# A hybrid attention layer on one core: the order of queries' and shares' parts, silu by tanh, and two products on GpSimd

## The chip, the core and the metric

The kernel runs on one NeuronCore of one Trainium2 chip. TensorE (PE) multiplies matrices into PSUM; VectorE (DVE), ScalarE (ACT) and GpSimd (POOL) work on tiles; SyncE (SP) issues most DMAs. Every engine has its own in-order queue of instructions; engines wait for one another on semaphores. The metric is the device time of one execution, in microseconds (us). Lower is better.

## The reference: what is computed

One encoder layer over 512 tokens and 16 learned "meta" tokens (528 rows), model width 2048, all in fp32:

```
hn   = RMSNorm(h); proj = hn @ w_in
qa, ka, va, ga, qb, kb, vb, gb = split(proj)
# mixer A: 8 query heads of 128 on 2 key/value heads
q, k = rope(rmsnorm(qa)), rope(rmsnorm(ka))
oA   = softmax(q k' / sqrt(128)) va
# mixer B: 8 heads, differential attention, two streams of 64
a    = softmax(s1 - slope*dist) - lambda * softmax(s2 - slope*dist)
oB   = rmsnorm(a vb) * (1 - lambda_init)
y    = concat(oA * silu(ga), oB * silu(gb)) @ w_out
out  = h + rmsnorm(y)             # real tokens only
```

silu(x) is x / (1 + exp(-x)), which equals (tanh z + 1) z with z = x / 2.

## The kernel before

**Precision by parts.** Every fp32 operand of a large product is split in two fp32r parts: a high part, which ACT writes as a copy (`hi`, L348), and a low part, which DVE writes as the difference (`lo`, L351). A product is then three matmuls: high by high, low by high, high by low (`three`, L198). The weights go through the same split in blocks of 128x1024 (`wsplit`, L153: tiles `st` to `wh`, `wl`).

**Stages.** (1) The first columns, with x arriving. (2) Mixer B: for each head h the columns of its gate, and the values, keys and queries of head h + 1 (`dense_T`, L224; tiles `pd` in four rotating PSUM banks), with the attention of head h woven in between. (3) Mixer A: its keys, values and two groups of queries. (4) The eight gates of mixer A, with the attention of mixer A woven in. (5) The output product (tiles `po`), with fewer products by sums and differences of blocks, the norm and the residual.

**What sets the order.** On PE the order is the program's. Class `Lanes` (L42) keeps a planned clock, to which every matmul adds its estimate. Work that waits for other engines is written as generators that yield a lag, such as `LAG["scB"]` = 3.0 us between two score products, and `poll` resumes one when the planned clock has passed its time; `finish` forces a task to its end. So the lags decide after which dense products an attention product stands. On ACT, DVE, POOL and SP the compiler's scheduler chooses the order by its own plan, by program order as priority. Splits of weights have a higher priority. Two things bind it: data dependences, and holds: `with tc.issue_after(i):` puts every instruction of the block that is on the engine of `i` behind `i` in that engine's queue. A hold adds no wait of its own; the instruction just cannot be placed earlier in its queue.

**Attention of mixer B** (`attention_B`, L516). For each block of 128 queries and each of two streams PE computes scores into the one PSUM tile `sc` from the queries' high part q and low part l and the keys' tile s, which holds the keys' high part in one half and the low part in the other. DVE adds the distance term, takes the extremum and empties `sc` (L533, tile mx). ACT takes Exp and the sum (L541), POOL scales the first stream (L546), DVE adds the second (L548) and turns blocks of 32x32 (L460). Two blocks of queries make a tile `pt`, which goes through DRAM and comes back regrouped (`regroup`, L464) as `pl`: the shares of attention, "p". `p_times_v` (L477) splits p into `ph` (ACT; one buffer) and `pl` (DVE) and the meta tokens' small `pm`, yields a lag (6.0 us in mixer B, 5.0 in A), and multiplies by the values into `pv`. ACT copies the result out (L554, L647). `finish_B` (L560) squares it, sums by PE, takes a square root on ACT (L573) and four reciprocals on DVE (L578), each 128x128 and held behind the newest maximum; then DVE multiplies the output by the roots (L581) and by the gate (L582), and SP stores it to the scratch `oscr` (L584). `queries_B` (L387) writes the queries' tiles: four high parts on ACT, four low parts on DVE, each of 64 partitions.

**Attention of mixer A** (`attention_A`, L609) is alike with one stream (scores L632 to L634, mxA L636, Exp L639, POOL L641); its queries' parts qh and qlA are written from a PSUM tile of transposes (L617, L618). The gate of head h - 1 is multiplied and stored while the gates' columns of later heads run (`silu_A`, L595; `gate_A`, L601); L602 is the product with the gate, L603 the store.

**Gates.** DVE multiplies the columns by the rows' norms (L437, L597), ACT applies Silu (L438, L598). Where ACT changes between functions of different tables, the compiler puts an ACT_TABLE_LOAD ahead.

Of the kernel before, what the change touches and what calls it, by code (L numbers as in the profile page):

```python
# [10 lines left out]
F32 = mybir.dt.float32  # L11
# [95 lines left out]
def kernel(ctx: ExitStack, tc: tile.TileContext, xT, xn, xm, w_s, w_t, w_q, w_o,  # L107
# [240 lines left out]
    def hi(dst, src):  # L348
        nc.scalar.activation(dst, src, AF.Copy)  # L349

    def lo(dst, src, h):  # L351
        nc.vector.tensor_tensor(out=dst, in0=src, in1=h.bitcast(F32), op=ALU.subtract)  # L352

    def keys_B(pss, after=nullcontext):
# [4 lines left out]
        with after():  # L359
            hi(s1[L], kf[L])  # L360
            hi(s2[U], kf[U])
            lo(s1[U], kf[L], s1[L])
            lo(s2[L], kf[U], s2[U])
# [22 lines left out]

    def queries_B(h, pss, after=nullcontext):  # L387
# [9 lines left out]
        with after():  # L397
            hi(to[0][L], qf[L])
            hi(to[2][U], qf[U])
            hi(to[0][U], qf[L])  # L400
            hi(to[2][L], qf[U])
            lo(to[1][L], qf[L], to[0][L])
            lo(to[3][U], qf[U], to[2][U])
            lo(to[1][U], qf[L], to[0][L])
            lo(to[3][L], qf[U], to[2][U])
# [28 lines left out]

    def gate(pss, name):
        g = gp.tile([P, SEQ], F32, name=name, tag="g", bufs=4)
        nc.vector.tensor_tensor(out=g, in0=pss[0], in1=rB[:, NM:], op=ALU.mult)  # L437
        nc.scalar.activation(g, g, AF.Silu)  # L438
        return g
# [37 lines left out]
    def p_times_v(regrouped, v, done, gate_of):  # L477
# [8 lines left out]
        with tc.issue_after(splits[-1][0].ins):  # L486
            hi(ph, pt)
            hi(pm[0:32], pf)
        lo(pl, pt, ph)
# [26 lines left out]
    def attention_B(h, qs, ks, v, v_task):  # L516
        o = ap.tile([P, SEQ], F32, name="oB", tag="f", bufs=4)
        last = None
        for half in range(2):
# [36 lines left out]
            if half == 0:  # L556
                yield LAG["scB"]
        over[h] = lanes.spawn(finish_B(h, o), LAG["fin"], last)

    def finish_B(h, o):  # L560
# [13 lines left out]
        for t in range(TT):  # L574
# [4 lines left out]
            if t == 1:  # L579
                yield LAG["scB"]  # L580
        nc.vector.tensor_tensor(out=o, in0=o, in1=sq, op=ALU.mult)  # L581
# [13 lines left out]
    def silu_A(pss):  # L595
        g = gp.tile([P, SEQ], F32, name="gt", tag="gt")
        nc.vector.tensor_tensor(out=g, in0=pss[0], in1=rB[:, NM:], op=ALU.mult)  # L597
        nc.scalar.activation(g, g, AF.Silu)  # L598
        return g

    def gate_A(h, g):  # L601
        nc.vector.tensor_tensor(out=oA[h], in0=oA[h], in1=g, op=ALU.mult)  # L602
# [6 lines left out]
    def attention_A(h, qn, q_task, k, k_task, v, v_task):  # L609
# [7 lines left out]
        hi(dealt(qh), by_token(tr))  # L617
        lo(dealt(ql), by_token(tr), dealt(qh))  # L618
# [5 lines left out]
        for half in range(2):  # L624
            pt = ap.tile([P, 1088], F32, name="pt", tag="pt")
            for t in (2 * half, 2 * half + 1):
# [12 lines left out]
                nc.scalar.activation(p, p, AF.Exp, scale=-1.0, bias=mx, accum_out=sm)  # L639
# [235 lines left out]
    heads, over = [None] * (2 * NH), [None] * (2 * NH)  # L875
# [5 lines left out]
    for h in range(NH):  # L881
# [7 lines left out]
        if h + 1 < NH:  # L889
            pss = dense_T(KEYS)  # L890
            if h:
                weigh()
                finish_head(h - 1)
# [369 lines left out]
```

## Time and profile before

| | us |
|---|---|
| runs shown: median (lowest to highest) | 899.06 (898.26 to 902.3) |
| the profiled execution, its own time | 901.28 |
| its span, first to last instruction | 899.5 |
| PE busy | 870.3 |
| DVE busy | 631.4 |
| ACT busy | 497.9 |
| POOL busy | 124.9 |

The granted clock of PE was 0.997 of full speed over the span. A row of a timeline reads: start, duration, engine, source line, operation, output<-inputs, shapes, count; in brackets the idle time of the engine before it and what ended it. A "q" behind an engine (SPq) is its sequencer. Names of tiles leave out the buffer's number, and a helper's line (L61, L349, L352) stands for all that call it, so the tile says which work it is. A matmul's end is modelled and overlaps the next one's start.

### The profile page before, as it was taken

Reading aid. Unit: us, or ns where it says so; the run is one execution under the profiler, and the core shown is the slowest. Engines: PE = TensorE matmul, PEld = TensorE weight load, DVE = VectorE, ACT = ScalarE, POOL = GpSimd, SP = SyncE. Lnnn points to the kernel's source line nnn. Section 1 sums busy time; section 2 is a strip of 40 time slices with the busy share of each in tenths; the row PEclk is TensorE's granted clock in tenths of the full one; section 3 lists DMA queues with packets and bytes.
Section 4 is the critical chain, followed back from the end, with each engine's and each line's share of the span. In section 5 each row is a group of like instructions: output and inputs, shape, how many; then the busy total and the mean of one; then the engine's idle time right before and its main releaser. Section 6 shows DMA issues by size and latency. Waiting matters only on the chain. (4 is left out here: it accounts for less than half of the span.)

```text
span 899.5 us, 14066 instructions
## 1 busy us (share of the span) xinstructions
PE 870.3 (97%) x5130; PEld 769.9 (86%) x5130; DVE 631.4 (70%) x1137; ACT 497.9 (55%) x844; POOL 124.9 (14%) x168
## 2 busy tenths in 40 slices
PE   9999999999999999999999999999999989999996
PEld 8999898998989889888898888987878778888884
DVE  6577786857857568485683485788666675886886
ACT  6565564637546474464654444656566555665561
POOL 0100220211011121101120021342111210000010
PEclk9999999999999999999999999999999999999998
DMA  9754979887696877868553334456566658989883
GB/s 336 262 163 144 236 216 258 201 233 194 198 260 155 247 212 222 241 170 238 143 181 94 105 94 149 144 168 182 170 181 217 181 167 283 317 275 308 272 276 152
DMA packets 80677, 185.49 MB, mean 206 GB/s; under 512 B 15136, under 2 KB 38560, under 8 KB 80224
## 3 DMA queue, kind: packets, MB, share of 16 engines
q1 hardware_dynamic: 75856, 167.81, 57.1%
q0 software_dynamic: 4608, 16.78, 11.3%
q8 instruction: 40, 0.66, 0.3%
q14 instruction: 29, 0.24, 0.1%
q10 hardware_dynamic: 144, 0.01, 0.0%
HBM read 158.34 MB, written 59.77 MB: 242 GB/s over the span
## 5 line engine op out<-in xcount | busy, mean ns | idle before, releaser
L61 PE MATMUL pd<-xh,wh 128*128 128x264 f32 (+1 forms) x992 | 325.8, 328 | 0.0
L61 PE MATMUL pd<-xl,wh 128*128 128x264 f32 (+1 forms) x992 | 323.1, 326 | 0.0
L61 PE MATMUL pd<-xh,wl 128*128 128x264 f32 (+1 forms) x992 | 322.7, 325 | 0.4 <-DVE wl L157 0.4
L156 ACT ACTIVATE wh<-st 128x1024 fp32r<-128x1024 f32 (+2 forms) x159 | 165.5, 1041 | 187.1 <-PE pd L61 92.4
L157 DVE TENSOR_TENSOR wl<-st,wh 128x1024 fp32r<-128x1024 f32 (+2 forms) x159 | 191.1, 1202 | 86.6 <-ACT wh L156 86.2
L61 PEld LDWEIGHTS pd<-xh,wl 128*128 128x128 f32 x992 | 186.5, 188 | 16.5 <-DVE wl L157 0.8
L61 PEld LDWEIGHTS pd<-xh,wh 128*128 128x128 f32 x992 | 186.8, 188 | 12.3 <-ACT wh L156 0.2
L61 PEld LDWEIGHTS pd<-xl,wh 128*128 128x128 f32 x992 | 187.0, 189 | 10.6
L541 ACT ACTIVATE p<-p,mx 128x528 f32<-128x528 f32 x64 | 47.1, 736 | 58.8 <-DVE mx L533 58.6
L61 PE MATMUL pd<-wh,xh 128*128 128x512 f32 x128 | 50.4, 394 | 0.0
L460 DVE STREAM_TRANSPOSE pt<-p 128x512 f32<-128x512 f32 x64 | 45.0, 702 | 7.1 <-POOL p L641 6.4
L61 PE MATMUL pd<-wh,xl 128*128 128x512 f32 x128 | 49.9, 390 | 0.0
L61 PE MATMUL pd<-wl,xh 128*128 128x512 f32 x128 | 49.9, 390 | 0.0
L639 ACT ACTIVATE p<-p,mxA 128x528 f32<-128x528 f32 x32 | 23.6, 737 | 46.2 <-DVE mxA L636 46.1
L533 DVE CUSTOM_DVE_ANT_0 p<-sc,dist 128x528 f32<-128x528 f32 x64 | 43.9, 686 | 4.7 <-PE sc L61 4.3
L821 POOL DMA_DIRECT2D ws<-in_w_o_dram x32 | 26.7, 834 | 146.0 <-DMA ws<-ws 64.0
L546 POOL TENSOR_SCALAR p<-p,sm 128x528 f32<-128x528 f32 x32 | 22.8, 711 | 173.2 <-DVE sm L543 164.9
L641 POOL TENSOR_SCALAR p<-p,smA 128x528 f32<-128x528 f32 x32 | 26.4, 826 | 119.1 <-DVE smA L640 97.9
L352 DVE TENSOR_TENSOR pl<-pl,ph 128x1024 fp32r<-128x1024 f32 x32 | 39.2, 1226 | 3.2 <-ACT ph L349 2.3
L61 PE MATMUL pv<-pl,vh 128*128 128x256 f32 x128 | 36.6, 286 | 4.4 <-DVE pl L352 4.4
L61 PE MATMUL sc<-s,q 128*128 128x264 f32 x128 | 35.3, 295 | 3.9 <-DVE mx L533 3.9
L548 DVE SCALAR_TENSOR_TENSOR p<-p,c 128x528 f32<-128x528 f32 x32 | 24.5, 766 | 20.7 <-POOL p L546 20.5
(223 smaller groups left out, 1569.8 us busy)
## 6 DMA issues: line engine op xcount, KB each, us to landing
st<-in_w_t_dram SPq DMA_DIRECT2D x82, 512.0 KB, 5.1
turn<-pt SPq DMA_DIRECT2D x32, 544.0 KB, 3.0
pl<-turn SPq DMA_DIRECT2D x128, 128.0 KB, 3.9
ws<-in_w_o_dram POOLq DMA_DIRECT2D x32, 512.0 KB, 8.1
st<-ws SPq DMA_DIRECT2D x32, 512.0 KB, 4.4
st<-in_w_o_dram SPq DMA_DIRECT2D x22, 512.0 KB, 4.3
ws<-in_w_o_dram SPq DMA_DIRECT2D x16, 512.0 KB, 6.7
ws<-ws SPq DMA_DIRECT2D x16, 512.0 KB, 7.0
```

Source lines behind the costliest of these rows:

```text
L61: self._add(self.nc.tensor.matmul(out, lhsT, rhs, start=start, stop=stop, **kw), us)
L156: splits.append((nc.scalar.activation(wh[:, c], st[:, c], AF.Copy), nc.vector.tensor_tensor(out=wl[:, c], in0=st[:, c], in1=wh[:, c].bitca ...
L157: nc.vector.tensor_tensor(out=wl[:, c], in0=st[:, c], in1=wh[:, c].bitcast(F32), op=ALU.subtract)))
L352: nc.vector.tensor_tensor(out=dst, in0=src, in1=h.bitcast(F32), op=ALU.subtract)
L460: nc.vector.transpose(pt[:, :1024].rearrange("p (m c t q) -> p c m t q", m=4, c=TT, t=2)[:, :, :, j], p[:, NM:].rearrange("p (c m q) -> p ...
L533: maxima.append(nc.vector.tensor_tensor_reduce(out=two(p), in0=sc[:, :, :HALF], in1=two(dist[:, w0:w0 + NT]), scale=-0.125 / slope(h), sca ...
L541: nc.scalar.activation(p2[m], p2[m], AF.Exp, scale=-1.0, bias=mx[:, m:m + 1], accum_out=sm[:, m:m + 1])
L546: nc.gpsimd.tensor_scalar(out=p2[0], in0=p2[0], scalar1=sm[:, 0:1], scalar2=1.0, op0=ALU.mult, op1=ALU.mult)
L548: nc.vector.scalar_tensor_tensor(out=p2[0], in0=p2[1], scalar=c2, in1=p2[0], op0=ALU.mult, op1=ALU.add)
L639: nc.scalar.activation(p, p, AF.Exp, scale=-1.0, bias=mx, accum_out=sm)
L641: nc.gpsimd.tensor_scalar(out=p, in0=p, scalar1=sm, scalar2=1.0, op0=ALU.mult, op1=ALU.mult)
L821: nc.gpsimd.dma_start(out=dst, in_=src, accum_op=ALU.add)
```

## The change

Five things change.

1. *Order of parts.* `keys_B` and `queries_B` write the parts of one stream, high then low, and then those of the other. The last high and the last low part of queries (of either mixer) are remembered in `q_last`, and those of shares in `p_last`.
2. *Holds.* In `p_times_v` ph and the high pm are held behind the last queries' high part traced so far (as well as behind the newest split of weights, as before), and pl behind the last queries' low part. In mixer A the Exp is held behind the last share's high part, the gates' silu behind both parts of the last share, and so are the splits of the output operands in `half_dead`. A hold binds instructions of the same engine alone.
3. *silu.* DVE computes z = 0.5 x r into the gate's tile, ACT writes tanh z back over the columns' PSUM tile, and DVE computes (tanh z + 1) z. Each gate has one DVE operation more, and the PSUM tile is read to the end of it.
4. *POOL.* The product of mixer B's output with the roots and that of mixer A's output with the gate go from DVE to POOL. The product with the gate in mixer B (L582 before) stays on DVE.
5. *finish_B.* It yields after each of the first three reciprocals (before, after the second alone). In the loop over heads, the finish of head h - 1 is forced only after the keys' columns; at the earlier place only its attention and its products with the values are forced (`products_B`).

```
--- before.py
+++ after.py
@@ -346,10 +346,10 @@
     L, U = slice(0, 64), slice(64, 128)
 
     def hi(dst, src):
-        nc.scalar.activation(dst, src, AF.Copy)
+        return nc.scalar.activation(dst, src, AF.Copy)
 
     def lo(dst, src, h):
-        nc.vector.tensor_tensor(out=dst, in0=src, in1=h.bitcast(F32), op=ALU.subtract)
+        return nc.vector.tensor_tensor(out=dst, in0=src, in1=h.bitcast(F32), op=ALU.subtract)
 
     def keys_B(pss, after=nullcontext):
         kf = ap.tile([P, NT], F32, name="kf", tag="tT")
@@ -357,10 +357,9 @@
         s1 = ap.tile([P, NT], F32R, name="s1", tag="s1")
         s2 = ap.tile([P, NT], F32R, name="s2", tag="s2")
         with after():
-            hi(s1[L], kf[L])
-            hi(s2[U], kf[U])
-            lo(s1[U], kf[L], s1[L])
-            lo(s2[L], kf[U], s2[U])
+            for s, a, b in ((s1, L, U), (s2, U, L)):
+                hi(s[a], kf[a])
+                lo(s[b], kf[a], s[a])
         return s1, s2
 
 
@@ -383,6 +382,17 @@
 
     def slope(h):
         return 2.0 ** (h - 2)
+
+
+    q_last, p_last = [None, None], [None, None]
+
+    @contextmanager
+    def behind_all(*ins):
+        with ExitStack() as stack:
+            for i in ins:
+                if i is not None:
+                    stack.enter_context(tc.issue_after(i))
+            yield
 
     def queries_B(h, pss, after=nullcontext):
         qf = ap.tile([P, NT], F32, name="qf", tag="tT")
@@ -395,14 +405,12 @@
         l2 = ap.tile([P, SEQ], F32R, name="l2", tag="ql", bufs=4)
         to, qf = [dealt(t) for t in (q1, l1, q2, l2)], by_token(qf)
         with after():
-            hi(to[0][L], qf[L])
-            hi(to[2][U], qf[U])
-            hi(to[0][U], qf[L])
-            hi(to[2][L], qf[U])
-            lo(to[1][L], qf[L], to[0][L])
-            lo(to[3][U], qf[U], to[2][U])
-            lo(to[1][U], qf[L], to[0][L])
-            lo(to[3][L], qf[U], to[2][U])
+
+            for q, l, a, b in (to[:2] + [L, U], to[2:] + [U, L]):
+                hi(q[a], qf[a])
+                q_last[0] = hi(q[b], qf[a]).ins
+                lo(l[a], qf[a], q[a])
+                q_last[1] = lo(l[b], qf[a], q[a]).ins
         return (q1, l1), (q2, l2)
 
     def values(pss, lag=LAG["vals"]):
@@ -432,11 +440,17 @@
 
         return (vh, vl, vm), lanes.spawn(turn(), lag)
 
+    def silu(pss, g):
+
+        nc.vector.scalar_tensor_tensor(out=g, in0=pss[0], scalar=0.5, in1=rB[:, NM:],
+                                       op0=ALU.mult, op1=ALU.mult)
+        nc.scalar.activation(pss[0], g, AF.Tanh)
+        nc.vector.scalar_tensor_tensor(out=g, in0=pss[0], scalar=1.0, in1=g, op0=ALU.add,
+                                       op1=ALU.mult)
+        return g
+
     def gate(pss, name):
-        g = gp.tile([P, SEQ], F32, name=name, tag="g", bufs=4)
-        nc.vector.tensor_tensor(out=g, in0=pss[0], in1=rB[:, NM:], op=ALU.mult)
-        nc.scalar.activation(g, g, AF.Silu)
-        return g
+        return silu(pss, gp.tile([P, SEQ], F32, name=name, tag="g", bufs=4))
 
 
     pv_last, maxima = [None], []
@@ -483,10 +497,11 @@
         pm = ap.tile([96, 2 * P], F32R, name="pm", tag="pm", bufs=1)
         pt = pl.bitcast(F32)
 
-        with tc.issue_after(splits[-1][0].ins):
+        with behind_all(splits[-1][0].ins, q_last[0]):
             hi(ph, pt)
-            hi(pm[0:32], pf)
-        lo(pl, pt, ph)
+            p_last[0] = hi(pm[0:32], pf).ins
+        with behind_all(q_last[1]):
+            p_last[1] = lo(pl, pt, ph).ins
         nc.gpsimd.tensor_scalar(out=pm[32:64], in0=pm[0:32].bitcast(F32), scalar1=1.0,
                                 scalar2=1.0, op0=ALU.mult, op1=ALU.mult)
         lo(pm[64:96], pf, pm[0:32])
@@ -555,6 +570,7 @@
                             LAG["pB"])
             if half == 0:
                 yield LAG["scB"]
+        products_B[h] = last
         over[h] = lanes.spawn(finish_B(h, o), LAG["fin"], last)
 
     def finish_B(h, o):
@@ -576,9 +592,9 @@
 
             with tc.issue_after(maxima[-1].ins):
                 nc.vector.reciprocal(out=sq[:, tq], in_=sq[:, tq])
-            if t == 1:
+            if t < TT - 1:
                 yield LAG["scB"]
-        nc.vector.tensor_tensor(out=o, in0=o, in1=sq, op=ALU.mult)
+        nc.gpsimd.tensor_tensor(out=o, in0=o, in1=sq, op=ALU.mult)
         nc.vector.scalar_tensor_tensor(out=gB[h], in0=o, scalar=sgc, in1=gB[h],
                                        op0=ALU.mult, op1=ALU.mult)
         nc.sync.dma_start(out=oscr[h // 2][h % 2], in_=gB[h])
@@ -594,12 +610,11 @@
 
     def silu_A(pss):
         g = gp.tile([P, SEQ], F32, name="gt", tag="gt")
-        nc.vector.tensor_tensor(out=g, in0=pss[0], in1=rB[:, NM:], op=ALU.mult)
-        nc.scalar.activation(g, g, AF.Silu)
-        return g
+        with behind_all(*p_last):
+            return silu(pss, g)
 
     def gate_A(h, g):
-        nc.vector.tensor_tensor(out=oA[h], in0=oA[h], in1=g, op=ALU.mult)
+        nc.gpsimd.tensor_tensor(out=oA[h], in0=oA[h], in1=g, op=ALU.mult)
         nc.sync.dma_start(out=oscr[4 + h // 2][h % 2], in_=oA[h])
         waiting[0] -= 1
 
@@ -614,8 +629,8 @@
         tr = ptr.tile([P, 512], F32, name="tr", tag="tr")
         for t in range(TT):
             transpose(tr[:, t * P:(t + 1) * P], qn[t][:, h % 4, :], ident)
-        hi(dealt(qh), by_token(tr))
-        lo(dealt(ql), by_token(tr), dealt(qh))
+        q_last[0] = hi(dealt(qh), by_token(tr)).ins
+        q_last[1] = lo(dealt(ql), by_token(tr), dealt(qh)).ins
         yield LAG["qA"]
         while not k_task[3]:
             yield 0.3
@@ -636,7 +651,8 @@
                 maxima.append(nc.vector.tensor_tensor_reduce(
                     out=two(p), in0=sc[:, :, :HALF], in1=two(zed[0][:, :NT]), scale=-ASCALE,
                     scalar=3.0e38, op0=ALU.add, op1=ALU.min, accum_out=mx))
-                nc.scalar.activation(p, p, AF.Exp, scale=-1.0, bias=mx, accum_out=sm)
+                with behind_all(p_last[0]):
+                    nc.scalar.activation(p, p, AF.Exp, scale=-1.0, bias=mx, accum_out=sm)
                 nc.vector.reciprocal(out=sm, in_=sm)
                 nc.gpsimd.tensor_scalar(out=p, in0=p, scalar1=sm, scalar2=1.0,
                                         op0=ALU.mult, op1=ALU.mult)
@@ -872,7 +888,7 @@
     v = values(pss)
     with behind():
         gB = [gate(first[2], "gB0")] + [None] * (NH - 1)
-    heads, over = [None] * (2 * NH), [None] * (2 * NH)
+    heads, over, products_B = [None] * (2 * NH), [None] * (2 * NH), [None] * NH
 
     def finish_head(h):
         lanes.finish(heads[h])
@@ -890,11 +906,14 @@
             pss = dense_T(KEYS)
             if h:
                 weigh()
-                finish_head(h - 1)
+
+                lanes.finish(heads[h - 1])
+                lanes.finish(products_B[h - 1])
             v = values(pss)
             ks = keys_B(dense_T(KEYS))
             if h:
                 weigh()
+                finish_head(h - 1)
             qs = queries_B(h + 1, dense_T(REAL))
     weigh()
     def start_heads(grp, qn, q_task, k, v):
@@ -957,7 +976,8 @@
                     with tc.issue_after(splits[-4][1].ins):
                         TTv(out=sd, in0=st, in1=sd, op=SUB)
                     st = sd
-                split(to[i], st)
+                with behind_all(*p_last):
+                    split(to[i], st)
 
     for h in range(NH):
         if h == 5:
```

More of the change, by code (lines that the diff above doesn't have):

```diff
@@ L359, in keys_B @@
         with after():
[L360 to L363, printed above, removed]
+            for s, a, b in ((s1, L, U), (s2, U, L)):
+                hi(s[a], kf[a])
+                lo(s[b], kf[a], s[a])
         return s1, s2
@@ L385, in slope, with behind_all @@
         return 2.0 ** (h - 2)
+    q_last, p_last = [None, None], [None, None]
+    @contextmanager
+    def behind_all(*ins):
+        with ExitStack() as stack:
+            for i in ins:
+                if i is not None:
+                    stack.enter_context(tc.issue_after(i))
+            yield
     def queries_B(h, pss, after=nullcontext):
@@ L397, in queries_B @@
         with after():
[L398 to L405, printed above, removed]
+            for q, l, a, b in (to[:2] + [L, U], to[2:] + [U, L]):
+                hi(q[a], qf[a])
+                q_last[0] = hi(q[b], qf[a]).ins
+                lo(l[a], qf[a], q[a])
+                q_last[1] = lo(l[b], qf[a], q[a]).ins
         return (q1, l1), (q2, l2)
@@ L484, in p_times_v @@
         pt = pl.bitcast(F32)
-        with tc.issue_after(splits[-1][0].ins):
+        with behind_all(splits[-1][0].ins, q_last[0]):
             hi(ph, pt)
-            hi(pm[0:32], pf)
-        lo(pl, pt, ph)
+            p_last[0] = hi(pm[0:32], pf).ins
+        with behind_all(q_last[1]):
+            p_last[1] = lo(pl, pt, ph).ins
         nc.gpsimd.tensor_scalar(out=pm[32:64], in0=pm[0:32].bitcast(F32), scalar1=1.0,
@@ L557, in attention_B @@
                 yield LAG["scB"]
+        products_B[h] = last
         over[h] = lanes.spawn(finish_B(h, o), LAG["fin"], last)
@@ L596, in silu_A @@
         g = gp.tile([P, SEQ], F32, name="gt", tag="gt")
-        nc.vector.tensor_tensor(out=g, in0=pss[0], in1=rB[:, NM:], op=ALU.mult)
-        nc.scalar.activation(g, g, AF.Silu)
-        return g
+        with behind_all(*p_last):
+            return silu(pss, g)
     def gate_A(h, g):
-        nc.vector.tensor_tensor(out=oA[h], in0=oA[h], in1=g, op=ALU.mult)
+        nc.gpsimd.tensor_tensor(out=oA[h], in0=oA[h], in1=g, op=ALU.mult)
         nc.sync.dma_start(out=oscr[4 + h // 2][h % 2], in_=oA[h])
@@ L638, in attention_A @@
                     scalar=3.0e38, op0=ALU.add, op1=ALU.min, accum_out=mx))
-                nc.scalar.activation(p, p, AF.Exp, scale=-1.0, bias=mx, accum_out=sm)
+                with behind_all(p_last[0]):
+                    nc.scalar.activation(p, p, AF.Exp, scale=-1.0, bias=mx, accum_out=sm)
                 nc.vector.reciprocal(out=sm, in_=sm)
@@ L874 @@
         gB = [gate(first[2], "gB0")] + [None] * (NH - 1)
[L875 removed]
+    heads, over, products_B = [None] * (2 * NH), [None] * (2 * NH), [None] * NH
     def finish_head(h):
@@ L892 @@
                 weigh()
-                finish_head(h - 1)
+                lanes.finish(heads[h - 1])
+                lanes.finish(products_B[h - 1])
             v = values(pss)
@@ L959, in half_dead @@
                     st = sd
-                split(to[i], st)
+                with behind_all(*p_last):
+                    split(to[i], st)
     for h in range(NH):
```

25 lines of the change are left out of this document (15 added, 10 removed).

## The prediction

> **What bounds the kernel now.** I read the page's first part, then the list of waits of TensorE (PE), then the timelines of PE, VectorE (DVE) and ScalarE (ACT) around the waits it names, and last the groups by line for what the change adds. All times are of the one profiled execution.
>
> ```profile
> span 899.5 us, 14066 instructions
> ...
> PE 870.3 (97%) x5130; PEld 769.9 (86%) x5130; DVE 631.4 (70%) x1137; ACT 497.9 (55%) x844; POOL 124.9 (14%) x168
> ```
>
> PE is the bound: 97% busy, with the number of its products fixed, and the change leaves that number alone. Only what PE waits for can be won. The list of waits (waiter and its line, what ended the wait: us in total, times, longest):
>
> ```profile
> PE sc L61 <- DVE l L352: 4.7, 4, 1.2
> PE pv L61 <- DVE pl L352: 4.4, 4, 1.5
> PE sc L61 <- DVE mx L533: 3.9, 7, 0.9
> PE sc L61 <- DVE qlA L352: 2.1, 4, 1.1
> PE sc L61 <- DVE mxA L636: 1.4, 1, 1.4
> PE sc L61 <- ACT qh L349: 1.1, 1, 1.1
> ...
> PE pv L61 <- ACT ph L349: 0.9, 2, 0.5
> ```
>
> These are 18.5 us in 23 waits: scores (sc) wait for the low parts of the queries (l, qlA) or for the maximum that empties the scores' PSUM (mx, mxA); the products with the values (pv) wait for the shares' parts (ph, pl). Each wait costs more than its row says, because matmuls overlap. The PE timeline at one of the four waits for l:
>
> ```profile
> 316.16 0.28 PE L61 MATMUL sc<-s,q 128*128 128x264 f32 x1
> 317.61 0.39 PE L61 MATMUL sc<-s,l 128*128 128x264 f32 x1 [1.17 <-DVE l L352]
> 317.83 0.29 PE L61 MATMUL sc<-s,q 128*128 128x264 f32 x1
> 317.96 0.29 PE L61 MATMUL sc<-s,l 128*128 128x264 f32 x1
> ```
>
> A product of this shape starts 0.13 us after the one before it (317.83 to 317.96). Here the start came 1.45 after, and the next one 0.22 after instead of 0.13: 1.32 + 0.09 = 1.41 lost against 1.17 shown, so 0.25 beyond each row. All 23 waits: 18.5 + 23 x 0.25 = 24.3 us, the most that removing PE's waits can bring.
>
> **Edit 1: order of queries' and shares' parts in mixer B.** What stood ahead of l in that head, on ACT and DVE, and the pv that needs the share which stood ahead:
>
> ```profile
> 312.10 1.07 ACT L156 ACTIVATE wh<-st 128x1024 fp32r<-128x1024 f32 x1 [2.18 <-PE pd L61]
> 313.06 1.05 ACT L349 ACTIVATE ph<-pl 128x1024 fp32r<-128x1024 f32 x1
> 314.01 2.58 ACT L349 ACTIVATE q<-qf 64x512 fp32r<-64x512 f32 x4
> ```
>
> ```profile
> 312.27 0.69 DVE L390 SCALAR_TENSOR_TENSOR qf<-pd,rB 128x512 f32<-128x512 f32 x1 [4.88 <-PE pd L61]
> 313.19 1.23 DVE L157 TENSOR_TENSOR wl<-st,wh 128x1024 fp32r<-128x1024 f32 x1 [0.23 <-ACT wh L156]
> 314.34 1.22 DVE L352 TENSOR_TENSOR pl<-pl,ph 128x1024 fp32r<-128x1024 f32 x1
> 315.47 2.88 DVE L352 TENSOR_TENSOR l<-qf,q 64x512 fp32r<-64x512 f32 x4
> ```
>
> ```profile
> 322.00 0.28 PE L61 MATMUL pv<-ph,vh 128*128 128x256 f32 x1
> ```
>
> The holds put ph and pl behind the queries' four high and four low parts, and the two streams' parts now alternate, so that the first stream's two low parts need two high ones, not four. ACT starts the first high part at 313.06; DVE is through wl at about 314.4 and writes the first stream's two low parts by 314.4 + 2.88/2 = 315.9. PE wants them 0.13 after 316.16, at 316.3. The wait goes, with 0.4 us to spare; the second stream's parts follow 1.4 us later. In exchange pl ends some 2.9 us after its 315.56, at 318.4, and its pv starts at 322.0: hidden, and without that cover each such head would pay up to 2.9. Four waits: 4.7 + 4 x 0.25 = **5.7 won** (0 to 5.7). The same alternation for the keys adds no instruction.
>
> **Edit 2: mixer B's roots.** Five of the seven waits for mx lie behind one pattern:
>
> ```profile
> 170.68 0.39 PE L61 MATMUL sc<-s,q 128*128 128x264 f32 x1 [0.51 <-DVE mx L533]
> ...
> 230.94 0.39 PE L61 MATMUL sc<-s,q 128*128 128x264 f32 x1 [0.21 <-DVE mx L533]
> ...
> 286.00 0.39 PE L61 MATMUL sc<-s,q 128*128 128x264 f32 x1 [0.68 <-DVE mx L533]
> ...
> 397.16 0.39 PE L61 MATMUL sc<-s,q 128*128 128x264 f32 x1 [0.90 <-DVE mx L533]
> ...
> 452.88 0.39 PE L61 MATMUL sc<-s,q 128*128 128x264 f32 x1 [0.87 <-DVE mx L533]
> ```
>
> ```profile
> 393.19 3.34 DVE L578 RECIPROCAL sq<-sq 128x128 f32<-128x128 f32 x4
> 396.45 0.64 DVE L533 CUSTOM_DVE_ANT_0 p<-sc,dist 128x528 f32<-128x528 f32 x1
> ```
>
> Four reciprocals, 3.34 us, run in one piece ahead of the maximum. After the change the plan yields after each, and each is held behind the newest maximum, so one (0.84) stands between two maxima; the maximum comes 2.5 us sooner, more than the longest of these waits. Won: 0.51 + 0.21 + 0.68 + 0.90 + 0.87 + 5 x 0.25 = **4.4** (0 to 4.4). The finish of a head ends two yields later; the move of its forced finish behind the keys' columns gives it room. The other two waits for mx I leave as they are.
>
> **Edit 3: silu by tanh, and holds in mixer A.** A stretch where both pv waits come from the gate:
>
> ```profile
> 699.99 0.39 ACT L647 ACTIVATE oA<-pv 128x256 f32<-128x256 f32 x1 [1.62 <-PE pv L61]
> ...
> 703.75 1.28 ACT L598 ACT_TABLE_LOAD   x1
> 705.05 0.63 ACT L598 ACTIVATE gt<-gt 128x512 f32<-128x512 f32 x1
> 705.59 1.04 ACT L349 ACTIVATE ph<-pl 128x1024 fp32r<-128x1024 f32 x1
> ```
>
> ```profile
> 705.71 0.69 DVE L602 TENSOR_TENSOR oA<-oA,gt 128x512 f32<-128x512 f32 x1 [1.78 <-ACT gt L598]
> 706.66 1.22 DVE L352 TENSOR_TENSOR pl<-pl,ph 128x1024 fp32r<-128x1024 f32 x1 [0.25 <-ACT ph L349]
> ```
>
> ```profile
> 706.68 0.39 PE L61 MATMUL pv<-ph,vh 128*128 128x256 f32 x1 [0.52 <-ACT ph L349]
> ...
> 707.94 0.38 PE L61 MATMUL pv<-pl,vh 128*128 128x256 f32 x1 [0.76 <-DVE pl L352]
> ```
>
> The one buffer of ph is free with the last share's products, which were read out at 699.99. The table load and the gate, 1.84 us (703.75 to 705.59), run on ACT ahead of ph all the same, and pl cannot start before ph. With the hold the gate comes after both parts, and ph can start at 703.75 or sooner: pl is then through at about 706.0 (1.04 + 1.22 later), ahead of both products that waited. Exp and the splits of the output operands get the same hold. Waits of pv: 4.4 + 0.9 + 6 x 0.25 = 6.8; I take **5.5** (0 to 6.8), as some shares may land too late for the order to matter. Of qlA, qh and mxA, 4.6 + 6 x 0.25 = 6.1, only those are touched where a share or a table load stands ahead, and the qh wait can turn into one for qlA: **2.0** (0 to 6.1).
>
> The table loads on ACT themselves:
>
> ```profile
> L438 ACT ACT_TABLE_LOAD x8 | 10.3, 1283 | 0.1
> ...
> L598 ACT ACT_TABLE_LOAD x7 | 9.0, 1283 | 0.1
> ```
>
> Fifteen loads stand at the gates, and most are paid again on the way back to Exp. If tanh lies in Exp's table, 15 to 30 loads go, 19 to 38 us of ACT; if not, none. No row here shows a tanh, and ACT is 55% busy, so this matters only through the waits already counted: without it about 1 us of the 2.0 is lost. The Trainium skill, "ScalarE: Activation LUTs", section "Table sets: the hidden batching unit", lists tanh in the set of exp. By it the full 38 us go from ACT and the sum stays.
>
> On DVE silu's second pass adds 16 operations of about 0.69 (as the row at 312.27), 11 us; the 16 products that go to POOL take as much away (0.69 in the row at 705.71). The gate's PSUM bank is held until that second pass; four banks rotate and the next user is over a column away, so I cost it at nothing; uncovered it is ACT's 0.63 plus 0.69 per gate.
>
> **Edit 4: sixteen products on POOL.** The nearest rows are POOL's one-tensor products of 128x528 and, for what DVE pays beside POOL, the small low part:
>
> ```profile
> L641 POOL TENSOR_SCALAR p<-p,smA x32: 704/706/2212, 542.1 to 717.7; 128x528 f32<-128x528 f32 x32
> ...
> L352 DVE TENSOR_TENSOR pm<-pt,pm x32: 416/418/732, 92.7 to 740.6; 32x256 fp32r<-32x256 f32 x32
> ```
>
> (minimum/median/maximum ns, first and last start.) With two tensors to read I take twice the median, 1.41 us; from below 0.71, from above the 2.21 of a product that shared its time with DVE. Behind these products on POOL's queue wait the products of p by its sum, which DVE's merge and then mx wait for; in DVE's queue the scaling by the gate (L582) now waits for POOL; on SP's queue the stores of both results wait longer, with the weights' loads behind them. Per product 0 to 1.41 reaches PE, 0 to 22.6 in all. Most fall where POOL is idle (14% busy): I take **3.0 lost**. The GPSIMD Engine Reference of the Trainium skill, section "Engine selection", advises VectorE for elementwise two-input work, POOL being about twice slower; that speaks against this edit, and by it each product is some 1.4 us, the value taken here from rows.
>
> The holds of mixer A can delay an Exp by ph and its small part; where that reaches PE I take **2.0 lost**, 0 to 1.04 for each of 16 shares (16.6) at the bound.
>
> **Sum.** 5.7 + 4.4 + 5.5 + 2.0 - 3.0 - 2.0 = 12.6 us. The profiled execution took 901.28 (899.5 of span and 1.8 around it), 2.2 above the median shown of 899.06. Against its own time: 888.7; as a median of runs **886.5 us**.
>
> **Rivals.**
> *Only mixer B is mended.* In mixer A the parts come late for other reasons (DVE work, not the order), the waits only move between ph, pl and qlA, and the costs remain: 10.1 - 5.0 = 5.1 won, 894.0. For it: most waits named there end on DVE, whose work is not reduced. Against it: the row at 703.75, where the gate is plainly ahead.
> *The order is not what set the waits.* The queue order follows the compiler's own plan; if that puts weights' splits (1.05 on ACT, 1.23 on DVE) into the places that come free, the waits change names and the time stays at 897 to 901, 899. For it: wl stands ahead of l at 313.19 too.
> *POOL and its waiters decide (slower).* At 1.41 each, with DVE standing at L582 and the products of p queued behind, all 16 reach PE: 22.6 lost and 2.0 for the holds, which the 17.6 of gains do not pay: 899.06 - 17.6 + 24.6 = 906. It decides from about 1.0 us exposed for each product ((17.6 - 2.0) / 16). Against it: POOL is idle 86% of the time, and nothing on PE needs the two results soon.
>
> **Chances.** Forecast (880 to 891) 0.52, mixer B alone 0.22, order without effect 0.14, POOL 0.12. About 0.5%, 4.5 us, is what a measurement of this kernel can tell from no change: faster is below 894.6, slower above 903.6. The forecast and 0.14 of the second case are faster, 0.66; 0.08 of the second, the third and a little of the fourth make same, 0.24; slower 0.10. The range runs from 878 (all 24.3 won, less POOL's 3.0) to 899, leaving out the POOL case and half of the third.
>
> **What would show it.** In the changed kernel's list of waits the rows for l and pl should be gone and that for mx at 1.5 or less; the reciprocals should appear singly between maxima; no table load should stand at the tanh; ph should come ahead of the gate. Wrong would be: rows of the same size for qlA, or new ones for sc on DVE; DVE waiting for POOL at L582 beyond 1 us a head; POOL products over 1.4 us.

## The result, and the profile after

| | before | after |
|---|---|---|
| runs beside each other: median (lowest to highest), us | 898.97 (897.77 to 902.75) | 891.19 (889.94 to 893.72) |
| the profiled execution, its own time, us | 901.28 | 890.24 |
| its span, us | 899.5 | 888.5 |
| granted clock of PE over the span | 0.997 | 0.993 |

The ratio is 0.9908, 95% interval 0.9881 to 0.9935: the kernel became 7.8 us faster by the medians and 11.0 by the profiled spans. Forecast were 12.6 won and 886.5. The median lies 0.2 us beyond the slow edge of the forecast's own band (880 to 891) and inside its range (878 to 899). The spans differ by 3.2 us more than the medians, because the profiled execution before is 2.3 above its median here and the one after 1.0 below.

The page's first part, kernel after:

```profile
span 888.5 us, 14071 instructions
...
PE 868.4 (98%) x5130; PEld 771.6 (87%) x5130; DVE 633.6 (71%) x1137; ACT 462.1 (52%) x816; POOL 150.1 (17%) x184
```

PE has the same 5130 products and is still the bound. ACT is busy 35.8 us less, POOL 25.2 more. The list of PE's waits, kernel after (waiter, what ended the wait: us in total, times, longest); L548 and L651 are the old L533 and L636:

```profile
PE sc L61 <- DVE qlA L352: 4.5, 3, 3.6
PE sc L61 <- DVE mx L548: 3.1, 8, 0.4
PE sc L61 <- DVE mxA L651: 1.5, 1, 1.5
```

The rows for l, pl, ph and qh are gone. The row for mx has eight waits for seven, with a total of 3.1 for 3.9, and that for qlA has more than doubled, with one wait of 3.6. These two rows hold what the forecast did not have. By stage (PE's timeline): the first score of mixer A starts at 531.47 instead of 538.74, and the first product of the output at 725.71 instead of 736.75. So 7.3 of the 11.0 us were won ahead of that score, and 3.8 in mixer A; the output stage takes as long as before.

**A new wait for the maximum.** Timelines of DVE and then of PE, kernel after, at the head whose wait for l the prediction showed:

```profile
311.85 2.80 DVE L352 TENSOR_TENSOR l<-qf,q 64x512 fp32r<-64x512 f32 x4
314.68 1.43 DVE L352 TENSOR_TENSOR pl<-pl,ph 128x1024 fp32r<-128x1024 f32 x1
316.14 0.42 DVE L352 TENSOR_TENSOR pm<-pt,pm 32x256 fp32r<-32x256 f32 x1
316.59 0.71 DVE L548 CUSTOM_DVE_ANT_0 p<-sc,dist 128x528 f32<-128x528 f32 x1
```

```profile
316.65 0.39 PE L61 MATMUL pd<-xh,wl 128*128 128x512 f32 x1
317.45 0.36 PE L61 MATMUL sc<-s,q 128*128 128x264 f32 x1 [0.42 <-DVE mx L548]
```

All four low parts now come first, as the change wants, and pl and the small pm come next, 1.43 + 0.42 us, ahead of the head's first maximum. The second pair of scores needs that maximum to empty `sc` and waits. Six heads have this wait, each of 0.39 to 0.42.

But the same work stood ahead of this maximum before, pl first and l behind it. DVE's timeline, kernel before:

```profile
318.83 0.71 DVE L533 CUSTOM_DVE_ANT_0 p<-sc,dist 128x528 f32<-128x528 f32 x1
```

Counted from the start of qf (312.27 before, 309.79 after), the maximum started 6.56 us later and now starts 6.80 later; most of these 0.24 are pl's, 1.43 for 1.22. The second pair of scores started 8.54 behind qf (at 320.81), because PE had stood for l first; now it starts 7.66 behind, even with its wait. So the maximum has hardly moved: PE, no longer held up at l, comes to it sooner. It is the same in all four heads that waited for l.

**The long wait for qlA.** PE's timeline, kernel after, in mixer A:

```profile
667.85 0.59 PE L61 MATMUL sc<-kh,qlA 128*128 128x264 f32 x1 [3.64 <-DVE qlA L352]
668.24 0.42 PE L61 MATMUL sc<-kh,qh 128*128 128x264 f32 x1
...
668.90 0.63 PE L61 MATMUL pd<-xh,wh 128*128 128x512 f32 x1
669.32 0.63 PE L61 MATMUL pd<-xl,wh 128*128 128x512 f32 x1
```

DVE's timeline ahead of it:

```profile
662.58 1.42 DVE L352 TENSOR_TENSOR pl<-pl,ph 128x1024 fp32r<-128x1024 f32 x1
...
664.56 0.67 DVE L445 SCALAR_TENSOR_TENSOR gt<-pd,rB 128x512 f32<-128x512 f32 x1
665.15 0.70 DVE L474 STREAM_TRANSPOSE pt<-p 128x512 f32<-128x512 f32 x1
...
665.87 0.67 DVE L474 STREAM_TRANSPOSE pt<-p 128x512 f32<-128x512 f32 x1
...
666.55 0.65 DVE L448 SCALAR_TENSOR_TENSOR gt<-pd,gt 128x512 f32<-128x512 f32 x1
667.12 0.68 DVE L352 TENSOR_TENSOR qlA<-tr,qh 128x512 fp32r<-128x512 f32 x1
```

The gate's two passes (L445, L448) and two turns of shares stand ahead of qlA. Nothing binds qlA to come before them, and it is the only work of these that PE needs at once. The products behind the wait start 0.42 apart (668.90 to 669.32); at 316.42 and 316.65 such products started 0.23 apart. That is the clock. Windows around this wait and around an earlier place, kernel after (columns: us, then busy time and count of PE, PEld, DVE, ACT and POOL, granted clock, DMA share, GB/s):

```profile
596.00:599.00 3.00, 1.19 (x7) 1.00 (x8) 3.00 (x9) 0.83 (x2) 0.00 (x0) 1.00 0.50 165
599.00:602.60 3.60, 3.60 (x14) 3.07 (x13) 3.60 (x11) 1.88 (x3) 2.03 (x2) 0.53 0.31 123
663.00:667.80 4.80, 1.21 (x7) 0.84 (x5) 4.74 (x10) 0.98 (x2) 1.22 (x2) 0.95 0.09 34
667.80:670.70 2.90, 2.85 (x10) 2.56 (x11) 0.72 (x2) 0.81 (x2) 0.75 (x1) 0.50 0.73 264
```

After each stand PE is granted about half its clock for some 3 us, and by the starts of its products it loses 1.2 (at 668) and 1.4 us (at 599) beyond the waits.

### The profile page after: what moved, and what is told of

It reads as the page before. It is cut to its first block, busy times and chain, and to the rows that moved or that the text cites. A ratio compares the mean times of both kernels' runs of the same rounds, so it can differ in the third digit from the quotient of the medians.

```text
span 888.5 us, 14071 instructions
## 1 busy us (share of the span) xinstructions
PE 868.4 (98%) x5130; PEld 771.6 (87%) x5130; DVE 633.6 (71%) x1137; ACT 462.1 (52%) x816; POOL 150.1 (17%) x184
## 5 line engine op out<-in xcount | busy, mean ns | idle before, releaser
L548 DVE CUSTOM_DVE_ANT_0 p<-sc,dist 128x528 f32<-128x528 f32 x64 | 44.4, 694 | 2.7 <-PE sc L61 2.3
L651 DVE CUSTOM_DVE_ANT_0 p<-sc,zed 128x528 f32<-128x528 f32 x32 | 22.4, 699 | 23.1 <-PE sc L61 22.9
```

What stands on the lines that cost most here:

```text
L548: maxima.append(nc.vector.tensor_tensor_reduce(out=two(p), in0=sc[:, :, :HALF], in1=two(dist[:, w0:w0 + NT]), scale=-0.125 / slope(h), sca ...
```

## The experiments

The theory under test: each part of the change moves a named wait of PE, by the order of the queues it touches. The rivals: the parts need one another; tanh, not the holds, mends mixer A; POOL's products cost nothing, or most of it. Ratios are to the kernel before on the same chip, with 95% intervals.

**Each part by itself.** `order_only`: changes 1 and 2 in mixer B and in `p_times_v`, nothing else.

```diff
-            hi(to[0][L], qf[L])
...
+            for q, l, a, b in (to[:2] + [L, U], to[2:] + [U, L]):
...
+        with behind_all(splits[-1][0].ins, q_last[0]):
+            hi(ph, pt)
...
+        with behind_all(q_last[1]):
+            p_last[1] = lo(pl, pt, ph).ins
```

> The kernel before with the new order of keys' and queries' parts, and the shares' parts held behind the queries' parts; nothing else. Theory (the wait moves): TensorE's four waits for l (4.7 us, 5.7 with what each costs beyond its row) are gone, but the share's low part, now behind l, stands ahead of the next maximum, and six heads wait some 0.4 us for mx instead, 3.7 us in all: 2 us faster, 897. Rival (independent): the waits for mx of the changed kernel come from the roots or POOL, and here only the five behind the reciprocals are left: 5.7 us faster, 893.

`roots_only`: change 5 alone.

```diff
-            if t == 1:
+            if t < TT - 1:
                 yield LAG["scB"]
...
-                finish_head(h - 1)
+                lanes.finish(heads[h - 1])
+                lanes.finish(products_B[h - 1])
...
                 weigh()
+                finish_head(h - 1)
```

> The kernel before with a yield after each of three reciprocals, and the finish of a head forced after the keys' columns; products stay on VectorE. Theory: the five waits for mx behind four reciprocals go, 4.4 us faster, 894.6; two short waits for mx are left. Rival: the reciprocals are spread but the maximum then waits for other work, the list still has 3 us or more for mx and the time stays within 1.5 us of before.

`gates_only`: tanh, and the holds behind the last share (those of Exp, gate and splits in mixer A).

```diff
-        nc.scalar.activation(g, g, AF.Silu)
+        with behind_all(*p_last):
+            return silu(pss, g)
...
+                with behind_all(p_last[0]):
+                    nc.scalar.activation(p, p, AF.Exp, scale=-1.0, bias=mx, accum_out=sm)
```

> The kernel before with silu by tanh and the holds behind the last share's parts (silu of mixer A, Exp of mixer A, the output operands' splits), but without the holds behind queries. Theory: this part alone removes the waits of pv (6.8 us) and of qh (1.3) and brings the one wait of 3.6 us for qlA with the slow clock after it (5 us in all): about 3 us faster, 896. Rival: the long wait for qlA comes from the hold of shares behind queries or from POOL, and here it is absent: 8 us faster, 891.

`pool_only`: the two products on POOL, nothing else.

```diff
-        nc.vector.tensor_tensor(out=o, in0=o, in1=sq, op=ALU.mult)
+        nc.gpsimd.tensor_tensor(out=o, in0=o, in1=sq, op=ALU.mult)
...
-        nc.vector.tensor_tensor(out=oA[h], in0=oA[h], in1=g, op=ALU.mult)
+        nc.gpsimd.tensor_tensor(out=oA[h], in0=oA[h], in1=g, op=ALU.mult)
```

> The kernel before with the two products on POOL, nothing else. Theory: the products take 1.3 to 2.1 us on POOL, and VectorE stands some 1 us a head at the product with the gate (L582), with splits of weights behind it but no maximum: within 1 us of before, 898 to 900. Rival: the standing VectorE reaches TensorE through mx, eight heads by 0.4 us or more: 3 us or more slower, 902.

| | median, us | ratio (interval) |
|---|---|---|
| order_only | 897.54 | 0.9985 (0.9968 to 1.0003) |
| roots_only | 897.73 | 0.9988 (0.9975 to 1.0000) |
| gates_only | 895.34 | 0.9955 (0.9940 to 0.9969) |
| pool_only | 904.24 | 1.0054 (1.0027 to 1.0080) |

The four add up to -0.15 - 0.12 - 0.45 + 0.54 = -0.18%; the whole change is worth -0.92%. So by the medians the parts need one another. The profiled spans alone would not say so: they fell by 1.8, 3.5, 5.6 and 0.7, 11.6 in all, beside 11.0 for the whole. But the one execution before that all are taken from was 2.2 above its median; less 2.2 each, they are 2.8 and 8.8. Of the expectations, that of `order_only` came in time, with fewer new waits than its six; `gates_only` came; those of `roots_only` (894.6) and `pool_only` (898 to 900) did not. PE's waits with the order alone:

```profile
PE sc L61 <- DVE mx L540: 4.4, 10, 0.9
...
PE sc L61 <- DVE l L352: 1.0, 1, 1.0
```

Three of the four waits for l went, and three new ones for mx came; the waits behind the four reciprocals stayed. With the roots alone, in the same list, the row for mx is gone, and that for l grew from four waits to six:

```profile
PE sc L61 <- DVE l L352: 7.0, 6, 1.2
```

In the two heads that are new, the plan has put pl ahead of the low parts of queries, as in the other four. DVE's timeline at one of them, with the roots alone:

```profile
204.74 1.22 DVE L352 TENSOR_TENSOR pl<-pl,ph 128x1024 fp32r<-128x1024 f32 x1
205.88 2.88 DVE L352 TENSOR_TENSOR l<-qf,q 64x512 fp32r<-64x512 f32 x4
```

In the kernel before, the four l of this head (from 204.20) stood ahead of pl (207.03). With the gates alone the rows for pl and ph are gone from the list of PE's waits, and mx has three waits (1.7 us) instead of seven; of mixer B this edit changes the gates' silu alone. The long wait for qlA is already there:

```profile
PE sc L61 <- DVE qlA L352: 4.5, 3, 3.6
```

With POOL's products alone a head's scaling stands for POOL up to 3.1 us (the list of DVE's waits):

```profile
DVE gB L582 <- POOL oB L581: 8.8, 7, 3.1
```

Its profiled execution took 900.56, at the low end of its runs (900.32 to 909.44), so that trace does not show the whole of the 4.9 us by which its median is slower (904.24 against 899.32). That is the rival's size (3 or more), though not by its path: the trace has four waits for mx, 2.9 us, not eight.

**The two parts of mixer B together.** `order_roots` is `order_only` with `roots_only`, both edits as above.

> The kernel before with both the order of queries' and shares' parts and the single reciprocals; silu, the holds of mixer A and VectorE's products as before. Theory (the two parts free each other: alone, each only hands its waits to the other's, l to mx and mx to l): the row for l is gone and that for mx at 3 us or less, mixer B loses 3.7 us against 11 us before, 6 us or more faster, 893 or less. Rival (the parts add): 1.3 + 1.1 = 2.4 us faster, 896.7.

Measured: 894.56, ratio 0.9929 (0.9908 to 0.9950), or 6.4 us where the two alone add up to 2.4. At the ends of the intervals the two readings still meet: the two alone are worth at most 0.57%, together at least 0.50%. PE's waits:

```profile
PE sc L61 <- DVE mx L540: 2.8, 7, 0.4
```

No row for l is left, and of mx only short waits. With the roots alone pl stood ahead of l in six heads, and the order puts it behind; with the order alone the waits behind the reciprocals stayed, and the roots take them away. The short waits for mx behind pl are here already, so they come from the order and not from POOL or the gates.

**POOL's products taken back.** `no_pool` is the changed kernel with both products on DVE again (the diff of `pool_only`, reversed).

> The changed kernel with the two products back on VectorE. Theory (POOL costs): the 7.9 us that VectorE stands for POOL at the product with the gate go, and of them 2 to 4 us reach TensorE or its spread of times: 1 to 4 us faster than the changed kernel, 887 to 890. Rival (POOL pays, by taking VectorE's work): the products stand ahead of mx or qlA again and the time is 1 to 3 us above the changed kernel's, 892 to 894.

Measured: 888.67, ratio 0.9864 (0.9842 to 0.9886), lower than with POOL by 0.44%, 4.0 us; the intervals overlap (0.9881 to 0.9886), and the medians as they stand differ by 2.5 (891.19 to 888.67). The profiled spans differ by 1.6 only (888.5 to 886.9), all of it ahead of mixer A's first score (531.47 to 529.83): in these traces the eight products of mixer A cost nothing on POOL. PE's waits:

```profile
PE sc L61 <- DVE mx L548: 2.4, 6, 0.4
```

Two of the eight waits for mx are gone, those that the changed kernel has at 333.9 and 388.3; the six behind pl stayed. The list of DVE's waits, its rows for POOL in mixer B, kernel after:

```profile
DVE p L563 <- POOL p L561: 27.0, 31, 2.9
DVE gB L598 <- POOL oB L597: 7.9, 7, 1.2
```

and `no_pool`:

```profile
DVE p L563 <- POOL p L561: 22.1, 28, 2.3
```

So in these rows DVE stands about 12.8 us less without POOL's products (7.9 + 4.9), and does 16 more operations (640.6 us busy against 633.6), at no cost in time.

**qlA first.** `ql_first` is the changed kernel with the queries' parts of mixer A at a higher priority.

```diff
-        q_last[0] = hi(dealt(qh), by_token(tr)).ins
-        q_last[1] = lo(dealt(ql), by_token(tr), dealt(qh)).ins
+        with tc.high_priority(400):
+            q_last[0] = hi(dealt(qh), by_token(tr)).ins
+            q_last[1] = lo(dealt(ql), by_token(tr), dealt(qh)).ins
```

> The changed kernel with a higher priority for mixer A's queries' parts, so that qlA stands ahead of the gate's two passes and the turns. Theory: the one wait of 3.6 us for qlA and the half clock behind it go, 4 to 5 us faster than the changed kernel, 886 to 887; the granted clock rises above 0.993. Rival: the wait is set by what stands before (split of weights, pl) and most of it stays or moves to the shares' parts: within 1.5 us of the changed kernel, 890 to 892.

Measured: 886.93, ratio 0.9841 (0.9814 to 0.9869), clear of the changed kernel's interval; span 884.3. PE's waits:

```profile
PE sc L61 <- DVE mx L548: 3.9, 10, 0.5
...
PE sc L61 <- DVE qlA L352: 1.1, 3, 0.6
```

The granted clock is back at 0.997. Of the span, 4.2 us came back, although mx has two waits more. From its first score (533.50) to the first product of the output (721.55), mixer A takes 188.1 us, against 194.2 in the changed kernel and 198.0 before: 6.2 were won there and 2.0 lost ahead of it. So that the gate's passes stand ahead of qlA is what ate into mixer A's gain.

**The maximum ahead of pl.** `mx_first` is the changed kernel with pl of mixer B traced 2.0 planned us later and held behind the newest maximum.

```diff
-        with behind_all(q_last[1]):
+        early = 2.0 if ab == "B" else 0.0
+        if early:
+            yield early
+        with behind_all(q_last[1], maxima[-1].ins if early else None):
             p_last[1] = lo(pl, pt, ph).ins
```

> The changed kernel with the shares' low part in mixer B traced 2.0 us of the plan later and held behind the newest maximum, so that the first maximum of a head stands ahead of it. Theory: the six waits of 0.4 us for mx at the head's start (3.7 us with what each costs beyond its row) go and none for pl comes: 3 us faster than the changed kernel, 888. Rival: the second maximum or pl is late instead and the time stays within 1 us, 890 to 892.

Measured: 892.44, ratio 0.9899 (0.9867 to 0.9931): not better than the changed kernel, as the rival had it. PE's waits:

```profile
PE sc L61 <- DVE mx L551: 7.1, 6, 2.7
```

The six short waits behind pl are gone, as expected, but others came, three of them of 1.4 to 2.7. What led to the longest, in the timeline of POOL and DVE:

```profile
269.85 0.84 POOL L840 DMA_DIRECT2D ws<-in_w_o_dram  x1 [7.97 <-DMA ws<-in_w_o_dram]
270.77 0.71 POOL L564 TENSOR_SCALAR p<-p,sm 128x528 f32<-128x528 f32 x1
...
271.51 0.77 DVE L566 SCALAR_TENSOR_TENSOR p<-p,c 128x528 f32<-128x528 f32 x1 [4.53 <-POOL p L564]
```

The scheduler's new order put a DMA issue of POOL's, which waited 8.0 us for an earlier transfer, ahead of the product that DVE needs. So this run shows that the six waits go when pl stands behind the maximum, and does not show what removing them is worth. That stays open.

**Tanh or the holds.** `silu_act` is the changed kernel with ACT's own Silu and the holds kept; `no_holds_A` keeps tanh and drops the three holds behind the last share.

```diff
-        nc.vector.scalar_tensor_tensor(out=g, in0=pss[0], scalar=0.5, in1=rB[:, NM:],
...
-        nc.scalar.activation(pss[0], g, AF.Tanh)
...
+        nc.vector.tensor_tensor(out=g, in0=pss[0], in1=rB[:, NM:], op=ALU.mult)
+        nc.scalar.activation(g, g, AF.Silu)
```

```diff
-        with behind_all(*p_last):
-            return silu(pss, g)
+        return silu(pss, g)
...
-                with behind_all(p_last[0]):
+                if True:
                     nc.scalar.activation(p, p, AF.Exp, scale=-1.0, bias=mx, accum_out=sm)
...
-                with behind_all(*p_last):
-                    split(to[i], st)
+                split(to[i], st)
```

> The changed kernel with ACT's own Silu in place of tanh and the second pass on VectorE; orders, holds and POOL's products stay. Theory (the order does the work, the tables little): 46 table loads or nearly so come back and 35 us or more of ACT's time with them, the waits of pv stay gone, the wait for qlA shrinks by the second pass (0.7) and the rest stays: within 2 us of the changed kernel, 889 to 893. Rival (the tables matter): loads ahead of ph, q and Exp bring waits for qh or mx of 3 us or more: 895 or more.

> The changed kernel without the three holds behind the last share's parts (silu of mixer A, Exp of mixer A, the output operands' splits). Theory (these holds remove the waits of pv): pv waits for pl and ph again, 3 to 5 us in the list, and the long wait for qlA becomes shorter, as the gate's passes move ahead of the share instead of ahead of qlA: 889 to 893. Rival (tanh removes them by taking the loads away): no wait of pv comes back and the time falls by the wait for qlA, 886 to 888.

Measured: `silu_act` 888.98, ratio 0.9864 (0.9835 to 0.9893), lower in its median than with tanh, with intervals that overlap; `no_holds_A` 898.12, ratio 0.9968 (0.9946 to 0.9990), two thirds of the gain gone. The waits of pv came back as its theory has it, but the time is far outside what either side expected (886 to 893). PE's waits without the holds:

```profile
PE sc L61 <- DVE mx L548: 5.3, 10, 1.8
PE pv L61 <- ACT ph L349: 3.0, 2, 2.5
...
PE pv L61 <- DVE pl L352: 2.1, 3, 1.1
```

Mixer A takes 201.0 us here (533.11 to 734.13) instead of 194.2, 6.8 more, which is what the forecast had as the most for pv. The span lost 1.6 more ahead of it, where mx has two waits more and the edit takes no hold away. With Silu and the holds there is no row for pv. The groups by line of ACT, its table loads, with Silu (busy, mean ns of one, idle before):

```profile
L553 ACT ACT_TABLE_LOAD x15 | 19.2, 1283 | 0.3
L446 ACT ACT_TABLE_LOAD x14 | 18.0, 1283 | 0.2
```

In the kernel after no load stands at the gates and seven at mixer B's Exp, so 18 are left of the 45 with Silu:

```profile
L589 ACT ACT_TABLE_LOAD x8 | 10.3, 1283 | 2.7 <-PE ss L61 2.6
L556 ACT ACT_TABLE_LOAD x7 | 9.0, 1283 | 0.1
```

So in mixer A the holds do the work; with them, 27 loads, 34.6 us of ACT, can be paid without a measurable loss.

**The best order found.** `ql_nopool` is the changed kernel with the edits of `ql_first` and `no_pool`; `ql_nopool_act` has ACT's Silu as well.

> The changed kernel with qlA first (a higher priority for mixer A's queries' parts) and with the two products on VectorE. Theory (the two are separate costs): 2.5 to 4 us for POOL and 5 us for qlA, 882 to 885, faster than either alone. Rival (VectorE's two more products stand ahead of mx in mixer B or of qlA): no faster than with qlA first alone, 886 to 888.

> The kernel with qlA first and VectorE's products (ratio 0.9807 to before), with ACT's own Silu in place of tanh and the second pass: only the orders, the holds and the single reciprocals are left of the change. Theory (tanh buys nothing, since with the holds no table load stands ahead of what TensorE waits for): ratio 0.978 to 0.984, 881 to 887 beside a before of 901. Rival (tanh pays once qlA is out of the way): ratio 0.985 or more, with waits for qh, ph or mx of 3 us more than with tanh.

Measured: 883.96, ratio 0.9807 (0.9780 to 0.9834), and 884.06, ratio 0.9826 (0.9805 to 0.9846): both clearly faster than the changed kernel and not to be told apart. Against `ql_first` the products on DVE are worth 0.34%, 2.5 us by the spans (884.3 to 881.8), again with intervals that overlap. PE's waits in `ql_nopool`:

```profile
PE sc L61 <- DVE mx L548: 2.9, 7, 0.5
...
PE sc L61 <- DVE qlA L352: 1.1, 3, 0.6
```

## Why the prediction was right, and where it was wrong

The sign, the bound and the two largest causes beside the order (the roots and pv) held; the order in mixer B and q's waits did not come as forecast. The measured 7.8 us lie below the 12.6. Against the profiled span, term by term:

| term | forecast, us | the runs |
|---|---|---|
| order in mixer B | +5.7 | +5.7 for l, -3.9 for mx |
| reciprocals singly | +4.4 | +4.4, and +1.2 for the two other waits of that row; in full only together with the order |
| pv in mixer A | +5.5 | +6.8, by the holds |
| q's waits in mixer A | +2.0 | about -2.0, and -1.4 by the clock at 599 |
| POOL | -3.0 | -1.6 by span, -4.0 by medians |
| holds of mixer A | -2.0 | 0 |

The column on the right, with POOL by span, comes to 9.2 of the 11.0 by which the span fell. The other 1.8 us have no row that I could name; about 1.5 of them lie ahead of mixer A's first score (7.3 won there, 5.8 by the terms). That the sum came near is in part luck: the order and q's waits fell short by 9.3 in all, and the other four terms came out better by 5.9.

**Order in mixer B: the wait went, and the next one in line came up.** The step that failed is the 5.7, the wait for l counted as won whole. The working asked only whether pv, which reads pl, can bear that pl ends 2.9 us later, and that was right: pv never waits. It did not ask what PE needs next: the second pair of scores, which need the head's first maximum, and l, pl and pm stand ahead of that in either order (6.56 us behind qf before, 6.80 after). While PE stood for l, that maximum was in time. The new price: at 317.45 the start came 0.80 after the one before it instead of 0.23; by the rule of 0.25 beyond each row, the six waits (2.4 us of rows) cost 2.4 + 1.5 = 3.9.

**Reciprocals.** All five waits named are gone, and so are the two left as they were (3.9 us in seven waits before, of which 3.17 were named; the six behind pl and the two of POOL's are new), 0.73 + 2 x 0.25 = 1.2 more. But the working had each edit winning alone, and alone each won little by the medians (0.9985 and 0.9988, with intervals that reach 1): with the roots alone, pl moved ahead of l in two more heads. The forecast did not see that this term needs the order; that both were made is why it came in full.

**pv in mixer A.** Right in size and in cause. That the holds, not the table loads, would decide was in the working ("this matters only through the waits already counted"), and the two runs bear it out. The Trainium skill, "ScalarE: Activation LUTs", section "Table sets: the hidden batching unit", has tanh in exp's set; the trace agrees, with no load at the tanh. Its rule to batch by set would remove 27 loads here, and by `silu_act` that is worth no time; ACT is busy 52 to 56%.

**q's waits: the step that failed most.** The 2.0 won rested on what stands ahead on ACT, a share or a table load. It left out DVE, where the gate now makes two passes: pl, both passes and two turns of shares all stand ahead of qlA. qh was ready at 663.4 by ACT; PE waited 3.64. Before, qlA and qh waited 3.2 us in five waits, with 0.25 each 4.5 lost; after, 4.5 in three, with 0.25 each 5.3, and 1.2 by the half clock: 2.0 lost instead of 2.0 won. `gates_only` shows the same row without any other edit, and `ql_first` takes it away. In `ql_first` mixer A takes 10.0 us less than before (188.1 to 198.0), more than the forecast's 5.5 + 2.0 - 2.0 for it. Of the prediction's four signs of being wrong three came: "rows of the same size for qlA", new waits "for sc on DVE" (the six for mx, whose row has 3.1 instead of at most 1.5), and POOL's products over 1.4 us.

**POOL.** The 3.0 lies between the two readings. Products on POOL, kernel after (minimum/median/maximum ns, first and last start):

```profile
L597 POOL TENSOR_TENSOR oB<-oB,sq x8: 1287/2130/2140, 131.4 to 495.4; 128x512 f32<-128x512 f32 x8
```

The estimate of 1.41 is right for a product alone and too low beside DVE's own two-input work. DVE's waits at L598, 1.0 a head (7.9 / 8), are at the bound named. The slower rival asked for 1.0 us exposed for each of 16 products; by the medians it is 4.0 / 16 = 0.25. PE needs neither result soon, as argued, and what is left reaches it through late maxima. Of the 4.9 us that the median of `pool_only` loses, most goes with the clock: six of its nine executions (902.98 to 909.44 us) had a granted clock of 0.990 to 0.994, the other three (900.32 to 902.81) one of 0.996 to 0.998, and of the 26 of the kernel before beside them only four had 0.994 or less. What takes the clock down there is open. It does not explain the medians of `no_pool`, whose executions lie where those of the changed kernel do (0.991 to 0.994).

**The rivals.** "Only mixer B is mended" gave 894.0; mixer A was mended in part (3.8 of the 11.0 us of span), and the measured time lies between that and the forecast. "The order is not what set the waits" falls by `no_holds_A` and `order_roots`. The holds' 2.0 for Exp did not come: mxA waits 1.5 as it did 1.4.

## What to carry to other kernels

Before a wait is counted as won, look at what the waiter needs next and what stands ahead of that: it will come there sooner (here the maximum, behind the same work as before). A hold orders the two instructions it names and nothing else, so the urgent work left unnamed (here qlA) can end up last; name it, or give it priority. Edits to one queue need not add up to their single effects, so measure them together as well as apart.

## What the runs showed of the hardware

**Half the clock after a stand.** After a wait of 3.64 us PE was granted 0.50 for 2.9 us. It was granted 0.53 for 3.6 us after two waits of 1.5 and 0.6 us between 596 and 599 as well, while the kernel before, with waits of 1.4 and 0.6 at the matching place (near 604), kept its clock. Windows, kernel before:

```profile
598.00:604.50 6.50, 5.12 (x33) 4.24 (x31) 5.82 (x16) 2.40 (x7) 2.52 (x3) 1.00 0.52 149
604.50:612.00 7.50, 6.87 (x40) 5.90 (x41) 7.47 (x19) 4.57 (x9) 2.44 (x3) 1.00 0.64 212
```

So the same short waits can cost 1.4 us more or not. Nor is it the kernel alone: the 26 executions of the kernel before beside `order_only` have mean granted clocks from 0.993 to 0.998. The Trainium skill, "TensorE: Matmul & The Clock Gate", section "Part 1: The HAM clock gate", has the clock halved after an idle window of some 3.4 us, with the window running free of the kernel. The wait of 3.64 agrees; the 0.53 after 1.5 + 0.6 us does not agree with a whole window of idling, and the runs do not settle what set it off.

**POOL and DVE hold each other up.** Timeline of POOL and DVE, kernel after:

```profile
342.64 1.16 DVE L157 TENSOR_TENSOR wl<-st,wh 128x1024 fp32r<-128x1024 f32 x1
...
342.81 2.14 POOL L597 TENSOR_TENSOR oB<-oB,sq 128x512 f32<-128x512 f32 x1 [3.74 <-DVE sq L594]
...
344.98 0.75 DVE L598 SCALAR_TENSOR_TENSOR gB<-oB,sgc,gB 128x512 f32<-128x512 f32 x1 [1.18 <-POOL oB L597]
```

POOL's product starts 0.17 us behind a two-input operation of DVE and takes 2.14 instead of 1.29: the 0.99 that DVE still had (342.81 to 343.80) and 1.15 of its own. The Trainium skill, "SBUF — State Buffer", section "Who interferes with whom", calls their shared port pair an exclusive lock that the first to start keeps for its whole instruction. The trace agrees: the second loses about what the first has left.
